# One hybrid decoder layer on one core: decode steps beside five heads, a norm product put later, the last squares taken by feature, and the values of seven heads turned by memory and VectorE

## The chip, the cores and the metric

One core of a Trainium2 chip runs the whole program. The metric is device time in microseconds of one launch. The kernel before was timed three times: 1744.43, 1745.99 and 1748.09 us, with the median 1745.99. One more execution was profiled and took 1747.35 us; its span in the profile, first to last recorded event, is 1745.6 us.

The engines are called as the profile calls them: PE (TensorE matmul; PEld is its weight load), DVE (VectorE), ACT (ScalarE), POOL (GpSimd) and SP (SyncE, which issues nearly all DMAs from one queue, in order).

## The reference, cut to what matters

One layer for a prompt of 1024 tokens and, with the same weights, eight requests that decode one token each from given states. Two mixers stand side by side, eight HGRN2 heads and sixteen Mamba-2 heads in two groups; then a gated MLP, and a last RMSNorm.

```python
h = rmsnorm(x, w['norm1_w'])
proj = h @ w['w_in']                       # 1024 x 6672
q_r, f_r, i_r, g_r, z, xbc_r, dt_r = jnp.split(proj, splits, axis=-1)
f = lb + (1.0 - lb) * jax.nn.sigmoid(f_r.astype(f32))
k = 1.0 - f
q = jax.nn.silu(q_r.astype(f32))
o_a, S_h_new = hgrn2_mix(heads(q), heads(k), heads(i_r.astype(f32)), heads(log_f), S_h.astype(f32))
o_a = rmsnorm(o_a, w['hgrn_norm_w']) * jax.nn.silu(heads(g_r).astype(f32))
...
y, S_s_new = ssd_scan(X * dt[..., None], A * dt, Bh, Ch, S_s.astype(f32))
y = y.reshape(Bsz, L, D_SSM) * jax.nn.silu(z.astype(f32))
y = rmsnorm(y.reshape(Bsz, L, SSM_GROUPS, -1), w['ssm_norm_w'].reshape(SSM_GROUPS, -1))
x = x + jnp.concatenate([o_a, y], axis=-1) @ w['w_out']
...
x = x + (jax.nn.silu(gate) * val) @ w['w_down']
y = rmsnorm(x, final_norm_w)               # after the layer
```

Here `hgrn2_mix` is, per head and token, S = diag(f) S + k v^T and o = q S; `v` is i_r. All is float32.

## The kernel before, in words

**Layout.** Features lie on the 128 partitions and tokens along the free axis: 1024 prompt tokens and, behind them, 8 decode tokens (NT = 1032). A projection tile is 128 features by three chunks of 344 tokens. Each float32 product is made of three products of rounded halves (weights wh and wl, activations hh and hl), and so one input job is 8 x 3 x 3 = 72 matmuls of 344 columns.

**Order on PE.** PE's queue is written out by hand. Jobs (`in_job`, L303: z0 to z7 for the gate of the Mamba part; f, q, v, sg for each head; then the output jobs) are generators that yield after each matmul. Beside them runs a stream: `ssd(g)` for the two Mamba groups, then `head(h, t)` for the heads. A stream yields weights, and `drive` (L279) makes a share of the remaining matmuls between two of its yields, until the job that it is driven to is done. So head h's small work is spread over the jobs of head h+1 (head 7's over output jobs), and a head takes about 62 us. `after(n, work)` (L242) puts work n matmul steps later. The queues of the other engines, and SP's, are ordered by a scheduler; `tc.issue_after(x)` asks that an instruction be queued behind x.

**A head (`head`, L934).** Its prompt part works in chunks of 128 tokens: products of q, k with powers of the forget gates fill the matrix `am` level by level (banks a0 to a6 in four stages, made by `near`: 64 or 32 pairs of products of only 16 to 64 columns), then per chunk the states SS (kv product, L1069; chain L1072 to L1074) and o = am v + q SS (L1094 on). For kv and o the values are wanted with tokens on the partitions, `vt`: eight PE transposes into two banks `vtp` (L945) and two ACT copies (L946) at the head's start. The norm of o follows: squares, `hms`, `rstd_of`, a round through memory (`hr_d`, `spread_rstd` 16 steps later), and 48 steps later `scale_out` (L1119): two DVE products sg = sg x norm and the store `mix_d<-sg`. The head's decode part loads two state tiles `Sh`, scales them with f on DVE (L959), adds k v, stores them, and takes `od` (PE, L1048) with `qb`; `odr` (L1051) is its copy. The loads of Sh for head h+1 can go out when od of head h has read the tiles.

**Decode steps of the Mamba part.** Sixteen heads make eight steps j. Each loads Sd (states), Bb and Cb (B and C spread over the partitions, 512 KB each), scales Sd on ACT (8 instructions), makes Bb x and Sd + Bb on DVE (1024 columns each), stores Sd, multiplies by Cb on POOL and sums on DVE. Steps 0 and 1 are made by `ssm_decode` in the z jobs z4 and z6, steps 2 to 7 by `decode_beside` (L677) in heads 1 to 6 in three parts: `load` behind the head's state store (L963), `front` behind odr, `back` behind the decode copy od (L1104). After the fourth step of a group `decode_gate` and, 80 steps later, `decode_norm` (dg, L735 to L737; xdk, L730) finish it, for group 1 at the start of head 7.

**The end.** The last rows of the down projection run by quarters of the tokens in the order 3, 0, 1, 2. Per quarter eight products dn are added to x on DVE (L1567); then, per 128 tokens, eight transposes `fin` (L1574), two ACT squares with a row sum (L1576), root and reciprocal, and two scales: one on DVE and one on ACT and POOL, or both on DVE in the last quarter (c == 2).

## Time and profile before

| what | us |
|---|---|
| runs: lowest, median, highest | 1744.43, 1745.99, 1748.09 |
| the profiled execution, and its span | 1747.35, 1745.6 |
| PE busy (share of the span) | 1704.6 (98%) |
| DVE busy | 1094.0 (63%) |
| ACT busy | 782.0 (45%) |
| POOL busy | 487.7 (28%) |
| granted TensorE clock, mean | 0.996 |

A row of the timeline gives the start, how long it took, the engine, the line, the operation, output and inputs by tile name, shapes, and in brackets the idle time of the engine just before, with what ended it. "x8" stands for eight of a kind together; a plain float32 matmul is recorded twice. A row of the groups gives the count, the busy time and the mean of one in ns. A row of windows gives, for a stretch, its length, then busy time and count for PE, PEld, DVE, ACT and POOL, the granted clock, the mean busy share of the 16 DMA engines, and GB/s. Of DMA queues it gives packets, MB and the share of 16 engines' time. Matmuls overlap, so a matmul's own duration is longer than the step from one start to the next.

### The profile page before, as it was taken

To read this page: it belongs to the slowest core of one execution; us is meant where nothing else is said; L and a number is where in the kernel's file an instruction comes from. 1 tells how busy PE (TensorE), PEld (TensorE's weight loads), DVE (VectorE), ACT (ScalarE), POOL (GpSimd) and SP (SyncE) were. 2 spreads that over 40 slices of the span, in tenths; PEclk is the share of its full clock that TensorE was granted. 3 is DMA by queue.
4 is the path that set the end of the run, shared out by engine and by line. 5 is a ranking of instruction groups with operands and counts; after the bars stand their busy time and mean duration, and the time that the engine had idled before them with its cause. 6 is when DMAs were issued, how large, how long until landed. Compare 5 with 4: busy or idle time off the path is not lost. (4 is left out here: it accounts for less than half of the span.)

```text
span 1745.6 us, 38507 instructions
## 1 busy us (share of the span) xinstructions
PE 1704.6 (98%) x16119; PEld 1657.3 (95%) x16119; DVE 1094.0 (63%) x1979; ACT 782.0 (45%) x1427; POOL 487.7 (28%) x501
## 2 busy tenths in 40 slices
PE   7999999999999999999999989999999999999998
PEld 7999999899989999999999989999999999999997
DVE  6668666555754655567746688666767667444545
ACT  7677685344445444445333464333334434111114
POOL 2102131110210211111122266666666664000002
PEclk9999999999999999999999999999999999999999
DMA  5354334533442443345437722222222226422212
GB/s 165 73 123 123 92 91 146 157 90 101 137 127 64 137 123 99 112 141 155 138 125 244 239 81 78 82 96 74 74 73 81 79 97 214 154 71 79 94 61 98
DMA packets 250036, 200.22 MB, mean 115 GB/s; under 512 B 47972, under 2 KB 221526, under 8 KB 249846
## 3 DMA queue, kind: packets, MB, share of 16 engines
q1 hardware_dynamic: 249574, 197.67, 37.4%
q8 instruction: 126, 2.06, 0.5%
q14 instruction: 48, 0.39, 0.1%
q0 software_dynamic: 288, 0.10, 0.0%
HBM read 155.16 MB, written 46.95 MB: 116 GB/s over the span
## 5 line engine op out<-in xcount | busy, mean ns | idle before, releaser
L93 PE MATMUL mm<-hl,wh 128*128 128x344 f32 x1248 | 405.2, 325 | 0.0
L93 PE MATMUL mm<-hh,wh 128*128 128x344 f32 x1248 | 404.9, 325 | 0.0
L93 PE MATMUL mm<-hh,wl 128*128 128x344 f32 x1248 | 402.0, 322 | 0.0
L93 PEld LDWEIGHTS mm<-hl,wh 128*128 128x128 f32 x1248 | 235.3, 189 | 4.8 <-issue 4.1
L93 PEld LDWEIGHTS mm<-hh,wh 128*128 128x128 f32 x1248 | 235.3, 189 | 4.0 <-issue 3.4
L93 PEld LDWEIGHTS mm<-hh,wl 128*128 128x128 f32 x1248 | 235.4, 189 | 1.4 <-issue 1.2
L199 ACT CAST wh<-ws 128x1024 fp32r<-128x1024 f32 x96 | 100.6, 1048 | 260.7 <-PE dn L93 134.8
L93 PE MATMUL ub<-uh,wh 128*128 128x258 f32 x704 | 200.1, 284 | 3.8 <-DVE fext L1432 2.7
L93 PE MATMUL ub<-ul,wh 128*128 128x258 f32 x704 | 199.5, 283 | 0.0
L93 PE MATMUL ub<-uh,wl 128*128 128x258 f32 x704 | 199.4, 283 | 0.0
L93 PE MATMUL dn<-ah,wh 128*128 128x256 f32 (+1 forms) x640 | 181.2, 283 | 2.0 <-DVE x L1549 2.0
L93 PE MATMUL dn<-al,wh 128*128 128x256 f32 (+1 forms) x640 | 180.6, 282 | 0.0
L93 PE MATMUL dn<-ah,wl 128*128 128x256 f32 (+1 forms) x640 | 180.1, 281 | 0.0
L201 DVE TENSOR_TENSOR wl<-ws,wh 128x1024 fp32r<-128x1024 f32 x88 | 109.7, 1247 | 93.3 <-ACT wh L199 92.6
L93 PE MATMUL mm<-mh,wh 128*128 128x258 f32 x512 | 146.5, 286 | 4.1 <-DVE x L1179 4.0
L93 PE MATMUL ua<-uh,wh 128*128 128x258 f32 x528 | 149.5, 283 | 0.8 <-DVE val L1444 0.4
L93 PE MATMUL ua<-ul,wh 128*128 128x258 f32 x528 | 149.2, 282 | 0.0
L93 PE MATMUL ua<-uh,wl 128*128 128x258 f32 x528 | 148.4, 281 | 0.0
L93 PE MATMUL mm<-ml,wh 128*128 128x258 f32 x512 | 145.3, 284 | 0.6 <-DVE ml L1136 0.6
L93 PE MATMUL mm<-mh,wl 128*128 128x258 f32 x512 | 144.9, 283 | 0.0
L93 PEld LDWEIGHTS ub<-uh,wh 128*128 128x128 f32 x704 | 133.6, 190 | 4.4 <-DVE fext L1432 2.9
L1382 DVE TENSOR_TENSOR wl<-wt,wh 128x512 fp32r<-128x512 f32 x88 | 89.4, 1035 | 74.2 <-ACT wh L1381 74.2
(373 smaller groups left out, 3987.4 us busy)
## 6 DMA issues: line engine op xcount, KB each, us to landing
ws<-in_w_in_dram SPq DMA_DIRECT2D x52, 512.0 KB
ws<-in_w_up_dram SPq DMA_DIRECT2D x44, 512.0 KB
ws<-in_w_out_dram SPq DMA_DIRECT2D x24, 512.0 KB
act_d<-val SPq DMA_DIRECT2D x22, 516.0 KB
al<-act_d SPq DMA_DIRECT2D x22, 516.0 KB
ws<-in_w_down_dram SPq DMA_DIRECT2D x22, 512.0 KB
ml<-mix_d SPq DMA_DIRECT2D x48, 172.0 KB
csb<-cs_d SPq DMA_DIRECT2D x32, 256.0 KB
```

The lines of the kernel that those rows point to most:

```text
L93: PE.matmul(out, lhsT, rhs, start=start, stop=stop)
L199: A.copy(wh[:, :n], ws[:, :n])
L201: V.tensor_tensor(wl[:, :n], ws[:, :n], wh[:, :n].bitcast(F32), op=ALU.subtract)
L1382: V.tensor_tensor(lo[:, cs], sums[name], hi[:, cs].bitcast(F32), op=ALU.subtract)
```

## The change

It has five parts.

1. **Values.** For heads 0 to 6 the job of v ends with four stores of v to memory `vb_d` (`v_end`), in pieces of 32 tokens, so that each block of 32 x 32 lands in the place of its transposed block. In the head the two `vt` tiles are loaded from there, queued behind the store of the second Sh, and two DVE transposes (of 32 x 32 blocks, in place), queued behind the odr copy, finish them. The PE transposes and ACT copies stay in head 7 only.
2. **Decode steps.** `decode_beside` runs in heads 1 to 5, for steps 3 to 7; step 2 is a third `ssm_decode`, and the three stand in z4, z5 and z6. Its load waits for the od matmul, its front is queued behind the od copy and square, its back behind `rstd_of`.
3. **Norm product.** `scale_out` of heads 0 to 6 is kept back and issued in the next head behind its odr copy.
4. **ssd's last yield** is 3.0 and not 1.0.
5. **The end.** In the last quarter (c == 2) ACT squares x by feature as each m is done, DVE adds the squares to `fa`, two matmuls of one column with ones give the sums of the rows, and one root and one reciprocal serve both halves; DVE makes three of the four scales and ACT with POOL the fourth.

```diff
@@ -686,8 +686,10 @@
         def load(behind):
-            with tc.issue_after(behind.ins):
-                SP.dma_start(d8(Sd), state_ssm[0, :, 2 * j:2 * j + 2].rearrange("b h p n -> (h p) b n"))
+            first_ = SP.dma_start(d8(Sd), state_ssm[0, :, 2 * j:2 * j + 2].rearrange("b h p n -> (h p) b n"))
+            tc.add_manual_dep(first_.ins, behind.ins.name,
+                              mybir.DependencyInfo(mybir.DependencyClass.Sync, mybir.DependencyReason.DATA))
+            with tc.issue_after(first_.ins):
                 SP.dma_start(Bb, bc_d[2 * g].rearrange("b n -> (b n)").unsqueeze(0).to_broadcast([P, T]))
@@ -734,7 +736,7 @@
         V.scalar_tensor_tensor(tmp, tmp, -0.5 / n, dst, op0=ALU.mult, op1=ALU.mult)
-        V.scalar_tensor_tensor(dst, tmp, 1.5, dst, op0=ALU.add, op1=ALU.mult)
+        return V.scalar_tensor_tensor(dst, tmp, 1.5, dst, op0=ALU.add, op1=ALU.mult)
@@ -747,8 +749,8 @@
                     acc.append(tl("g", "gacc"))
-                if g and i % 2 == 0:
-                    ssm_decode(0, i // 2)
+                if g and i < 3:
+                    ssm_decode(0, i)
@@ -818,7 +820,7 @@
         ssd_back(parts, NC - 1)
-        yield 1.0
+        yield 3.0
         ssm_state_out(g)
@@ -848,6 +850,7 @@
     vd_d = dram.tile([H, ND, P], F32, name="vd_d")
+    vb_d = dram.tile([H - 1, P, NC, P], F32, name="vb_d")
     hr_d = dram.tile([H, 4, 256], F32, name="hr_d")
@@ -918,6 +921,12 @@
+        def v_end():
+            for b in range(4):
+                SP.dma_start(vb_d[h, :, :, 32 * b:32 * b + 32].rearrange("(a j) c r -> j c a r", j=32),
+                             t["v"][32 * b:32 * b + 32, :T].rearrange("j (c a r) -> j c a r", a=4, r=32))
+
+        ends = {"f": f_end, "v": v_end if h < H - 1 else None}
         for n, off, func in (("f", OFF_F, AF.Tanh), ("q", OFF_Q, AF.Silu), ("v", OFF_I, AF.Copy),
@@ -929,17 +938,23 @@
             else:
-                in_job(f"{n}{h}", off + h * P, evict, begin, f_end if n == "f" else None)
+                in_job(f"{n}{h}", off + h * P, evict, begin, ends.get(n))
         return t
+
+    unscaled = []
...
         f, k, q, v, sg = (t[n] for n in ("f", "k", "q", "v", "sg"))
-        step_ = decode_beside((h + 1) // 4, (h + 1) % 4) if 1 <= h <= 6 else None
-
+        step_ = decode_beside((h + 2) // 4, (h + 2) % 4) if 1 <= h <= 5 else None
+
+        later_vt = []
         dps = bank("vd", "nx")
...
         for hf in range(2):
+            if h < H - 1:
+                later_vt.append((vt[hf], vb_d[h, :, 4 * hf:4 * hf + 4, :]))
+                continue
             ps = bank("vtp")
@@ -958,10 +973,12 @@
             G.tensor_tensor(Sd, Sd, vb, op=ALU.add)
-            kept_ = SP.dma_start(hgrn_sample[0, bs, h].rearrange("b k v -> k b v"), d4(Sd))
+            stored = SP.dma_start(hgrn_sample[0, bs, h].rearrange("b k v -> k b v"), d4(Sd))
             Sds.append(d4(Sd))
-        if step_:
-            step_[0](kept_)
+
+        for dst, src in later_vt:
+            with tc.issue_after(stored.ins):
+                SP.dma_start(dst.rearrange("p (c n) -> p c n", n=P), src)
@@ -1041,16 +1058,22 @@
             A.copy(am[b:b + 32, :, b + 32:b + 64], c32(ps[:, :256])[b:b + 32])
-        turned_ = A.copy(am[0:64, :, 64:P], p6[0:64, :].rearrange("p (c t) -> p c t", t=64))
+        A.copy(am[0:64, :, 64:P], p6[0:64, :].rearrange("p (c t) -> p c t", t=64))
...
             g = b % 4
-            mm(ops[32 * g:32 * g + 32, :P], qb[:, b, :], Sds[b // 4][:, b % 4, :], start=(b < 4), stop=(b >= 4))
+            oded = PE.matmul(ops[32 * g:32 * g + 32, :P], qb[:, b, :], Sds[b // 4][:, b % 4, :], start=(b < 4), stop=(b >= 4))
+        if step_:
+            step_[0](oded)
         odr = small.tile([P, P], F32, tag="odr", bufs=1, name=nm("odr"))
-        held = V.tensor_copy(odr, ops[:, :P])
-        if step_:
-            step_[1](held, turned_)
+        copied = V.tensor_copy(odr, ops[:, :P])
+        if h < H - 1:
+            for hf in range(2):
+                with tc.issue_after(copied.ins):
+                    V.transpose(vt[hf], vt[hf])
+        if unscaled:
+            unscaled.pop()(copied)
         yield 3.5
@@ -1079,10 +1102,10 @@
         held = V.tensor_copy(od[:, 0, :], dps[:, :ND])
-        A.activation(od[:, 1, :], dps[:, :ND], AF.Square)
+        turned_ = A.activation(od[:, 1, :], dps[:, :ND], AF.Square)
+        if step_:
+            step_[1](held, turned_)
         yield 3.2
-        if step_:
-            step_[2](held)
@@ -1105,7 +1128,9 @@
         nt = half("nt")
-        rstd_of(nt[:, 0:256], nt[:, 256:512], ps[:, :256], P)
+        held = rstd_of(nt[:, 0:256], nt[:, 256:512], ps[:, :256], P)
+        if step_:
+            step_[2](held)
         SP.dma_start(hr_d[h], nt[::32, 0:256])
@@ -1116,13 +1141,19 @@
-        def scale_out():
+        def scale_out(behind=None):
             for hf in range(2):
-                V.tensor_tensor(sg[:, hb[hf]], sg[:, hb[hf]], sq[hf], op=ALU.mult)
+                with ExitStack() as order_:
+                    if behind is not None:
+                        order_.enter_context(tc.issue_after(behind.ins))
+                    V.tensor_tensor(sg[:, hb[hf]], sg[:, hb[hf]], sq[hf], op=ALU.mult)
             SP.dma_start(mix_d[h], sg[:, :NT])
...
         after(16, spread_rstd)
-        after(48, scale_out)
+        if h < H - 1:
+            unscaled.append(scale_out)
+        else:
+            after(48, scale_out)
@@ -1560,32 +1591,63 @@
         wd.append((hi, lo))
+    def opened(t0, n):
+        tb = [bank("fin"), bank("fin")]
+        return t0, n, tb, [tl("t", "ot"), tl("t", "ot")], keep.tile([P, 6], F32, tag="ss", bufs=4, name=nm("fss"))
+
+    def turned(o, ks):
+        t0, n, tb, ot, ss = o
+        for k in ks:
+            PE.transpose(tb[k // 4][:n, blk[k % 4]], xT[k][:, t0:t0 + n], ident)
+
+    def scaled(o, i, r, shared):
+        t0, n, tb, ot, ss = o
+        ds = slice(i * 512, (i + 1) * 512)
+        if shared:
+            A.activation(ot[i][:n], tb[i][:n, :], AF.Copy, scale=r)
+            G.tensor_tensor(ot[i][:n], ot[i][:n], fw[:n, ds], op=ALU.mult)
+        else:
+            V.scalar_tensor_tensor(ot[i][:n], tb[i][:n, :], r, fw[:n, ds], op0=ALU.mult, op1=ALU.mult)
+        SP.dma_start(y_prompt[0, t0:t0 + n, ds] if t0 < T else y_sample[:, 0, ds], ot[i][:n])
+
     for c in (3, 0, 1, 2):
         cs = quarters[c]
+        parts_ = [(t0, min(P, cs.stop - t0)) for t0 in range(cs.start, cs.stop, P)]
+        acc_ = tl("us", "fa")[:, :256]
         for m in range(KT):
...
             V.tensor_tensor(xT[m][:, cs], xT[m][:, cs], ps, op=ALU.add)
...
+            if c == 2:
+                q_ = tl("us", "fq")[:, :256] if m else acc_
+                A.activation(q_, xT[m][:, cs], AF.Square)
+                if m:
+                    V.tensor_tensor(acc_, acc_, q_, op=ALU.add)
+        if c == 2:
+            os_ = [opened(t0, n) for t0, n in parts_]
+            for o in os_:
+                turned(o, range(KT - 1))
+            sums = psmm.tile([P, 512], F32, tag="mm", name=nm("fs"))
+            for b in range(2):
+                mm(sums[:, b:b + 1], acc_[:, blk[b]], ones[:, 0:1])
+            for o in os_:
+                turned(o, range(KT - 1, KT))
+            r = os_[0][4]
+            A.activation(r[:, 0:2], sums[:, 0:2], AF.Sqrt, bias=epsc, scale=1.0 / DM)
+            V.reciprocal(r[:, 2:4], r[:, 0:2])
+            for b, i in ((0, 0), (0, 1), (1, 0), (1, 1)):
+                scaled(os_[b], i, r[:, 2 + b:3 + b], (b, i) == (1, 1))
+        else:
+            for t0, n in parts_:
+                o = opened(t0, n)
+                tb, ot, ss = o[2:]
+                turned(o, range(KT))
...
+                for i in range(2):
+                    scaled(o, i, ss[:n, 3:4], i == 1)
```

How the queues change. First VectorE's queue in the middle of the fourth head, from the decode copy odr to the last state step, before (sg_6165 is that head's gate tile, Sd_6300 and Bb_6301 its Mamba step, Sh_7128 and Sh_7136 the next head's states):

```order
L1051 COPY odr_6825<-od_6816 128x128
L698 TENSOR_TENSOR Bb_6301<-Bb_6301,xdd_6299 128x1024
L950 TENSOR_TENSOR qb<-eye_796,q_6614 128x8x8
L702 TENSOR_TENSOR Sd_6300<-Sd_6300,Bb_6301 128x1024
L959 TENSOR_TENSOR Sh_7128<-Sh_7128,f_6354 128x512
L959 TENSOR_TENSOR Sh_7136<-Sh_7136,f_6354 128x512
L1072 COPY SS_6917<-kv_6918 128x128
L1074 SCALAR_TENSOR_TENSOR SS_6917<-SS_6917,tt_6345,kv_6918 128x128 x2
```

and the same place of the changed kernel (sg_5386 is the gate tile of the head before):

```order
L1070 COPY odr_6838<-od_6825 128x128
L1074 STREAM_TRANSPOSE vt_6343<-vt_6343 128x512
L1074 STREAM_TRANSPOSE vt_6344<-vt_6344 128x512
L1149 TENSOR_TENSOR sg_5386<-sg_5386,sq_6222 128x512
L1149 TENSOR_TENSOR sg_5386<-sg_5386,sq_6234 128x512
L965 TENSOR_TENSOR qb<-eye_796,q_6623 128x8x8
L974 TENSOR_TENSOR Sh_7138<-Sh_7138,f_6377 128x512
L974 TENSOR_TENSOR Sh_7146<-Sh_7146,f_6377 128x512
L1095 COPY SS_6921<-kv_6922 128x128
L1097 SCALAR_TENSOR_TENSOR SS_6921<-SS_6921,tt_6368,kv_6922 128x128
```

The transposes and the held-back products stand where Bb and Sd stood; Bb is now behind the second and Sd behind the fifth of the seven state steps.

SyncE's queue at that place, before, where Sd, Bb and Cb had gone out right behind the stores of Sh of the head's first part:

```order
L961 DMA out_dram<-Sh_6324 128x4x128
L961 DMA out_dram<-Sh_6332 128x4x128
L690 DMA Sd_6300<-in_state_ssm_dram 128x8x128
L691 DMA Bb_6301<-bc_d 128x1024
L693 DMA Cb_6302<-bc_d 128x512
L693 DMA Cb_6303<-bc_d 128x512
L196 DMA ws_6968<-in_w_in_dram 128x8x128
L182 DMA Sh_7128<-in_state_hgrn_dram 128x4x128
L182 DMA Sh_7136<-in_state_hgrn_dram 128x4x128
```

and of the changed kernel (from the first Sh on, all wait for od):

```order
L976 DMA out_dram<-Sh_6357 128x4x128
L981 DMA vt_6343<-vb_d 128x512
L981 DMA vt_6344<-vb_d 128x512
L182 DMA xd_6394<-in_x_sample_dram 8x512
L182 DMA xd_6395<-in_x_sample_dram 8x512
L196 DMA ws_6990<-in_w_in_dram 128x8x128
L182 DMA Sh_7138<-in_state_hgrn_dram 128x4x128
L689 DMA Sd_6337<-in_state_ssm_dram 128x8x128
L693 DMA Bb_6338<-bc_d 128x1024
L695 DMA Cb_6339<-bc_d 128x512
L695 DMA Cb_6340<-bc_d 128x512
L1150 DMA mix_d<-sg_5386 128x1032
```

The next row is the second Sh (Sh_7146): the two loads of Sh, which stood together, now have the Mamba step's loads and the store of the gate tile between them.

VectorE's queue at the start of head 7, before (dg and xdk finish the Mamba group, sg_8532 is head 6's gate tile):

```order
L1009 TENSOR_TENSOR v_9181<-q_8961,f_8715 128x1024
L1121 TENSOR_TENSOR sg_8532<-sg_8532,sq_9331 128x512
L986 TENSOR_TENSOR tt_9472<-f_8715 128x512
L1121 TENSOR_TENSOR sg_8532<-sg_8532,sq_9343 128x512
L201 TENSOR_TENSOR wl_9478<-ws_9476,wh_9477 128x1024
L1136 TENSOR_TENSOR ml_9489<-ml_9489,mh_9485 128x344 x2
L986 TENSOR_TENSOR tt_9473<-tt_9472 128x256
L735 SCALAR_TENSOR_TENSOR dg_9319<-dgs_9545,dg_9319 128x8
L980 TENSOR_TENSOR k_8952<-k_8952,f_8715 128x512
L736 SCALAR_TENSOR_TENSOR dg_9319<-dg_9319 128x8
L981 TENSOR_TENSOR v_9181<-v_9181,f_8715 128x512
L737 SCALAR_TENSOR_TENSOR dg_9319<-dg_9319 128x8
```

and of the changed kernel:

```order
L1026 TENSOR_TENSOR v_9179<-q_8968,f_8714 128x1024
L1003 TENSOR_TENSOR tt_9463<-f_8714 128x512
L1003 TENSOR_TENSOR tt_9464<-tt_9463 128x256
L1003 TENSOR_TENSOR tt_9464<-tt_9464 128x128
L201 TENSOR_TENSOR wl_9469<-ws_9467,wh_9468 128x1024
L1167 TENSOR_TENSOR ml_9480<-ml_9480,mh_9476 128x344 x2
L1033 TENSOR_TENSOR amc_9465<-a_1069_9544,eyec 128x256
L1003 TENSOR_TENSOR tt_9464<-tt_9464 128x64
L997 TENSOR_TENSOR k_8959<-k_8959,f_8714 128x512
L998 TENSOR_TENSOR v_9179<-v_9179,f_8714 128x512
```

The two products on sg and the three steps on dg are gone from here, and three short squarings tt stand ahead of k.

PE's queue differs only in the first Mamba rows of the start, in the 56 transposes that are gone, in the group's closing product (in head 6 and not in head 7), and at the very end.

28 lines of the change are left out of this document (6 added, 22 removed).

## The prediction

> **What bounds the kernel now.** I read four things in this order: the page's busy shares, the list of everything TensorE waits for, the timeline around those waits, and the DMA queues inside them.
>
> ```profile
> span 1745.6 us, 38507 instructions
> PE 1704.6 (98%) x16119; PEld 1657.3 (95%) x16119; DVE 1094.0 (63%) x1979; ACT 782.0 (45%) x1427; POOL 487.7 (28%) x501
> ```
>
> PE is busy 98% of the span. So only two things can shorten it: fewer PE instructions, or a shorter wait of PE; work moved on VectorE, ScalarE or SyncE's queue counts only where PE waits for it. PE's waits in the part that the change touches (waited for: total, times, longest):
>
> ```profile
> PE a L93 <- issue: 5.2, 3, 2.5
> PE sT L636 <- DVE S L611: 2.3, 1, 2.3
> PE a L93 <- DVE q L981: 2.3, 1, 2.3
> PE mm L93 <- DVE ml L1136: 0.6, 1, 0.6
> ```
>
> That is 10.4 us in six waits, and they are what an edit off PE can win here.
>
> **Values by memory: the transposes that go.** One head's start on PE, then all of them, and the ScalarE copies behind them:
>
> ```profile
> 372.58 0.27 PE L940 MATMUL vd<-ident,v 128*8 128x128 f32 x1
> 372.69 1.03 PE L945 MATMUL vtp<-ident,v 128*128 128x128 f32 x8
> 373.48 0.40 PE L93 MATMUL mm<-hh,wh 128*128 128x344 f32 x1
> L945 PE MATMUL vtp<-ident,v 128*128 128x128 f32 x64 | 8.3, 272 | 0.0
> L946 ACT COPY vt<-vtp 128x512 f32<-128x512 f32 x16 | 8.6, 594 | 0.0
> ```
>
> The 272 ns are the time in flight of one transpose, not its price: eight occupy 1.03 us. The price is start to start. From 372.58 (vd) to the next projection row at 373.48 stand nine transposes in 0.90; the ninth projection row starts somewhat late, by the 0.40 of its own row, so I take 0.11 each, 0.87 for eight. Seven heads lose theirs: **-6.1 us** (by 0.10 it would be -5.6, by 0.12 -6.7). The two ScalarE copies per head (2 x 594 ns) hide today beside projections and win nothing.
>
> The Trainium skill, "TensorE: Matmul & The Clock Gate", Part 4, gives a transpose about 275 ns in a kernel's context, and the trace's mean of 272 agrees. Multiplied by 56 this would be an estimate of -15.4 us, but the starts in the row above are 0.11 apart, so I go by those.
>
> What comes instead runs beside PE: four stores of 128 KB and two loads of 256 KB a head, and two VectorE transposes. A store in such 128-byte pieces exists already (x_prompt to its copy), and so does the transpose:
>
> ```profile
> 54.00:56.00 2.00, 2.00 (x20) 2.00 (x18) 2.00 (x2) 1.72 (x2) 0.00 (x0) 1.00 0.74 116
> L901 DVE STREAM_TRANSPOSE xs<-xs 128x512 f32<-128x512 f32 x16 | 11.2, 704 | 10.5 <-DMA xs<-xb_d 10.5
> ```
>
> 116 GB/s at a DMA share of 0.74 make 155 GB/s at full share: 512 KB take 3.4 us. They start when the job of v ends, over ten us before the next head begins, and the values are first read by that head's kv product some 40 us into it; the loads go out 14 us into it. I see no wait there: 0. The 2 x 0.70 on VectorE come up below.
>
> **The three waits named "issue".** These are the largest item, and the diff has no line about them. Their rows, and the DMA queues (packets, MB, share) of the whole run, of 512.0 to 519.5 and of 519.5 to 521.0:
>
> ```profile
> 390.26 0.19 PE L93 MATMUL a<-q,f 128*32 128x32 f32 x1 [0.77 <-issue]
> 518.60 0.76 PE L93 MATMUL a<-q,f 128*32 128x32 f32 x64
> 519.21 0.55 PE L93 MATMUL a<-v,k 128*16 128x16 f32 x48
> 522.25 0.29 PE L93 MATMUL a<-v,k 128*16 128x16 f32 x16 [2.49 <-issue]
> 649.51 0.21 PE L93 MATMUL a<-v,k 128*16 128x16 f32 x2 [1.92 <-issue]
> q8 instruction: 126, 2.06, 0.5%
> ```
> ```profile
> q1 hardware_dynamic: 2331, 2.02, 94.7%
> ```
> ```profile
> q8 instruction: 1, 0.02, 3.7%
> ```
>
> 2.06 MB in 126 packets are 16 KB each, and PE's 2 x 16119 instructions are 126 x 256: the packets are PE's instructions, 256 at a time. The counts between the stalls say the same:
>
> ```profile
> 390.20:522.20 132.00, 129.47 (x1784) 123.88 (x1783) 76.78 (x138) 57.52 (x98) 14.71 (x10) 1.00 0.42 125
> 522.20:649.50 127.30, 125.34 (x1656) 120.27 (x1656) 73.17 (x142) 60.89 (x106) 17.77 (x12) 0.99 0.38 111
> ```
>
> 1784 + 1783 = 3567 and 1656 + 1656 = 3312 recorded instructions; with the 16 or 17 semaphore instructions of PE between them these are 14 x 256 and 13 x 256. So each stall sits on a packet's border. It is a border that falls at the end of the burst of small "a" products (64 and 64 pairs of weight load and product, in some 1.3 us without the stall), at a moment when the data queue is full: for 7.5 us at a share of 0.95 no instruction packet moved at all, then one came and PE went on. The data are the store of Sh, Sd, Bb, Cb and a weight tile, 2.4 MB issued 14 us into heads 2 and 4.
>
> The change touches both conditions. Every head has 16 PE instructions fewer, so the border at 522.25 moves 48 instructions on (the burst had 32 left) and that at 649.51 80 on (4 left): both leave the burst. And 1.5 MB of the data (Sd, Bb, Cb) go out behind od instead, so the queue empties some 4.5 us sooner. Other borders come into bursts: I counted all of them in the changed order, and six have 5.1 to 5.6 us from the border before to the end of their packet, against the 4.7 to 5.5 of those that stalled; the queue is nearly empty at four. I take 5.2 of stalls gone and 0.6 new: **-4.6** (ends: 0, all reappear, and -5.2).
>
> The Trainium skill, "Runtime: NRT & Kernel Launch", Instruction fetch mechanics, has the same blocks of 16 KiB, 256 instructions, but calls the cost of crossing one mostly hidden. By that rule the stalls would have another cause and stay, and the sum would be 4.6 us higher.
>
> **Head 7 is relieved.** VectorE at its start, with the wait that PE has there:
>
> ```profile
> 813.30 0.69 DVE L1121 TENSOR_TENSOR sg<-sg,sq 128x512 f32<-128x512 f32 x1
> 818.78 1.00 DVE L736 SCALAR_TENSOR_TENSOR dg<-dg 128x8 f32<-128x8 f32 x1
> 820.31 1.25 DVE L737 SCALAR_TENSOR_TENSOR dg<-dg 128x8 f32<-128x8 f32 x1
> 821.82 0.63 DVE L730 SCALAR_TENSOR_TENSOR xdk<-xdk,vcol,dg 128x8 f32<-128x8 f32 x4
> 822.97 0.68 DVE L981 TENSOR_TENSOR q<-v,tt 128x512 f32<-128x512 f32 x1
> 823.80 0.93 PE L93 MATMUL a<-q,f 128*32 128x32 f32 x53 [2.33 <-DVE q L981]
> ```
>
> VectorE has no pause from 812 to 824, and the q that PE waits for is at its end. Two norm products (2 x 0.6 start to start) go behind od, and the group end of the decode (0.9 + 1.2 + 0.5) to head 6, whose start has the same work but one output job less beside it. That is 3.8 us out of a chain that is 2.33 late; the three tt halvings that now come ahead cost some 0.5. So -2.3, and the 0.63 for ml goes with the norm product: **-2.9** (ends 0 and -2.9). The same 2.1 now stand at head 6's start, where PE had no wait: 0, at most +1.
>
> **The decode behind od.** Here the change adds a danger. The rows of head 3:
>
> ```profile
> 595.38 0.64 PE L93 MATMUL od<-Sh,qb 128*32 128x128 f32 x16
> 595.86 0.94 SPq L182 DMA_DIRECT2D Sh<-in_state_hgrn_dram  x2
> 605.76 0.29 DVE L1072 COPY SS<-kv 128x128 f32<-128x128 f32 x1 [3.35 <-PE kv L93]
> L702 DVE TENSOR_TENSOR Sd<-Sd,Bb 128x1024 f32<-128x1024 f32 x6 | 7.4, 1225 | 0.4 <-ACT Sd L701 0.3
> 613.93 0.39 PE L93 MATMUL o<-q,SS 128*128 128x128 f32 x2
> 512.00:519.50 7.50, 7.50 (x146) 7.04 (x147) 4.54 (x8) 4.23 (x6) 0.00 (x0) 1.00 0.95 269
> 760.00:773.00 13.00, 13.00 (x322) 12.49 (x321) 8.74 (x14) 5.47 (x8) 2.73 (x2) 1.00 0.69 204
> ```
>
> SyncE issues now, behind od: Sh, Sd, Bb, two Cb, the store of sg, and only then the second Sh, 2.62 MB in all where it was 0.5. VectorE's queue has the scaling of that Sh ahead of COPY SS, so the whole chain of states waits for it. At the 269 GB/s of just such loads it lands 9.7 us on, with one to two for the first to start at 606.6 to 607.6; the scaling takes 1.2, so COPY SS starts near 608.3 instead of 605.76. From there SS6 comes 4.5 us later (six small steps of some 0.3, and Bb and Sd of 1.1 each between them): 612.8. PE reads it for its last product of o, 0.45 behind the row at 613.93, at 614.4. So 1 to 2 us are left, and I count **+0.3** for the five heads. VectorE's time beside it balances: two transposes and two norm products (2.7) for Bb and Sd (2.4), under a pause of 3.35. The third ssm_decode in the z jobs brings ScalarE and SyncE a wait for Sd where none bound PE; ends 0 and 3, I take **+0.5**. The yield of 3.0 in place of 1.0 changes no row of PE's order at sT, so the 2.3 there stay.
>
> **The end.** Before, behind the last dn:
>
> ```profile
> 1736.21 0.42 DVE L1567 TENSOR_TENSOR x<-x,dn 128x256 f32<-128x256 f32 x1 [0.28 <-PE dn L93]
> 1736.64 0.60 ACT L1576 ACTIVATE ot<-fin 128x512 f32<-128x512 f32 x1 [1.91 <-PE fin L1574]
> 1738.95 1.41 DVE L1586 SCALAR_TENSOR_TENSOR ot<-fin,fss,fw 128x512 f32<-128x512 f32 x2
> 1741.05 1.41 DVE L1586 SCALAR_TENSOR_TENSOR ot<-fin,fss,fw 128x512 f32<-128x512 f32 x2
> ```
>
> ScalarE's row squares (four of 0.60 and their sums) and two rounds of root and scale go. If only the last dn counted, x at 1736.21, square, add, two products, root, reciprocal and three scales of 0.7 would end 5.0 behind it against 6.3 now: -1.3. But VectorE gets seven adds of 0.36 in the last quarter, beside eight x adds of 0.36, two scales of 0.75 and small ones: 7.7 us from 1731.2, where PE takes 5. It comes out some 2 late: **+0.65** (ends -1.3 and +1.5).
>
> **The sum**, against the profiled execution's 1747.35 (1.75 outside the span, 1.36 above the median of 1745.99): -6.1 - 4.6 - 2.9 + 0.3 + 0.5 + 0.65 = -12.1, which is 1735.2 in the profile and 1733.8 as a median. I predict **1734**, 0.7% faster.
>
> **Rivals.** (a) The instruction stalls reappear at other borders: five heads now have a fuller queue, though behind od, where no burst stands, which speaks against it; or they have a cause that the change doesn't touch, and stay. Then 4.6 are missing: 1738 to 1740. The Trainium skill's page named above stands for the second of these. (b) The second Sh comes at the 204 GB/s of the row at 760, whose share is only 0.69: 12.8 + 1.5 us, 1.6 too late, five times: +8, or 1743. (c) The other side: the queue behind od gives only 158 GB/s, as it moved over 595.9 to 606.0 before (at a share of 0.57, so mostly unasked, which speaks against it). Then Sh lands after 18.1 us, 5.4 beyond the 12.7 that it has, in five heads: +27, or 1761. It turns slower than before when it lands later than about 15 us behind od, 2.4 a head. (d) VectorE bounds the end: at most 1737.
>
> **Chances.** Forecast, with (d) in it: 0.54, 1731 to 1738. (a) 0.20; (b) 0.14; (c) 0.12. The measurement tells about 0.2%, 3.5 us: faster below 1742.5 is 0.54 + 0.20, same is nearly all of (b), slower is (c). The range of eight in ten reaches from the forecast's low end, 1731, over (a) and most of (b) to 1745.
>
> **What would show it.** PE's count falls by 56 transposes and no "issue" wait over 1 us stands in the bursts of heads 2 and 4: the first two steps. No wait of PE on q near 820: the third. A wait of o on SS in heads 1 to 5, with VectorE's Sh waiting for its load: (b) or (c), and the prediction is wrong. An "issue" wait elsewhere, again a multiple of 256 from the others: (a). The span's end less the last dn tells the tail.

## The result, and the profile after

| | lowest | median | highest | runs |
|---|---|---|---|---|
| before, us | 1744.43 | 1745.76 | 1752.49 | 6 |
| after, us | 1749.70 | 1753.99 | 1756.36 | 6 |

The changed kernel is slower: 1.0043 of the kernel before, 95% interval 1.0026 to 1.006. The forecast was 1734 with a range of 1731 to 1745: the change went the other way, and the time lies above the range. The profiled execution of after took 1756.36, its span is 1754.6, 9.0 more than before's.

The page's head, after:

```profile
span 1754.6 us, 38477 instructions
PE 1705.6 (97%) x16067; PEld 1656.6 (94%) x16067; DVE 1098.2 (63%) x1998; ACT 779.4 (44%) x1416; POOL 483.3 (28%) x502
```

PE has 52 rows fewer (56 transposes less, 4 rows of the products fs more), yet its busy time rose by 1.0. So it did less work in more time, and waited more besides. What PE waited for (total, times, longest), after:

```profile
PE mm L93 <- ACT x L1208: 4.8, 1, 4.8
PE cst L346 <- DMA rt<-in_state_conv_ffn_dram: 4.5, 1, 4.5
...
PE a L93 <- issue: 2.8, 3, 1.4
...
PE sT L636 <- DVE S L611: 2.5, 1, 2.5
...
PE mm L93 <- issue: 1.4, 2, 1.1
...
PE fin L1601 <- DVE x L1619: 1.1, 2, 0.7
...
PE o L93 <- DVE SS L1097: 0.7, 1, 0.7
```

Two waits of over 4 us are new, and neither is in the prediction. The wait of 2.33 for q in head 7 is down to 0.21, as forecast. "Issue" came down from 5.2 to 2.8 + 1.4 = 4.2, not to 0.6. The two new ones in PE's timeline, after:

```profile
518.26 0.42 PE L346 MATMUL cst<-ident,rt 16*128 16x16 f32 x4 [4.50 <-DMA rt<-in_state_conv_ffn_dram]
...
833.77 0.58 PE L93 MATMUL mm<-mh,wh 128*128 128x258 f32 x1 [4.80 <-ACT x L1208]
```

**The first: rows of a state, late in SyncE's queue.** `rt` are small loads of the MLP's convolution state that PE turns (L346) between two heads' work. SyncE's queue around them, before:

```profile
498.20 0.34 SPq L182 DMA_DIRECT2D rt<-in_state_conv_ffn_dram  x1
...
502.46 0.43 SPq L182 DMA_DIRECT2D rt<-in_state_conv_ffn_dram  x1
...
508.07 3.22 SPq L961 DMA_DIRECT2D out_dram<-Sh  x2
...
514.27 0.44 SPq L182 DMA_DIRECT2D rt<-in_state_conv_ffn_dram  x1
```

and after:

```profile
510.05 3.52 SPq L976 DMA_DIRECT2D out_dram<-Sh  x2
513.62 0.99 SPq L981 DMA_DIRECT2D vt<-vb_d  x2
514.65 1.37 SPq L182 DMA_DIRECT2D rt<-in_state_conv_ffn_dram  x3
```

Before, the rows went out one at a time, two of them ahead of the stores of Sh. After, three stand together behind the stores of Sh (which wait for POOL's sums, so SyncE's queue stands still until 510) and behind the new loads of `vt`. They went out at 514.65 and PE had them at 518.26. The diff asks only that vt stand behind the store of Sh; in an in-order queue whatever the scheduler puts behind vt is held back with it. How the 4.5 divide isn't shown: the stores of Sh hold the rows until 513.6, the loads of vt take another 1.0 of SyncE's queue, and while the rows were under way (514.65 to 518.2) the DMA engines were busy at a share of 0.75.

**The second: ScalarE's evictions behind its casts.** The output job beside head 7 needs `ml` (the mixed heads, from memory), which ScalarE casts to `mh`. ScalarE, after:

```profile
829.00 0.94 ACT L1166 CAST mh<-ml 128x344 fp32r<-128x344 f32 x2 [3.00 <-DMA ml<-mix_d]
830.98 1.44 ACT L1166 CAST mh<-ml 128x344 fp32r<-128x344 f32 x3 [1.04 <-DMA ml<-mix_d]
...
833.36 0.36 ACT L1208 COPY x<-mm 128x258 f32<-128x258 f32 x1
```

`COPY x<-mm` empties the bank that PE waits for, and it is a third of a microsecond of work. It stands behind five casts that wait for loads of ml, and behind two copies for the head. In before, the Mamba part's store `mix_d<-xdk` goes out at 822.47, behind head 7's stores of Sh, and the loads of ml follow from 823.69 on. In after it went out at 765.98, a head earlier, and SyncE issues the loads of ml at 817.6, at 822.1 and from 825.3 on: before, between and behind the two stores of Sh, which wait for POOL. That the earlier store is why the scheduler placed the loads and casts among the evictions is my reading of the two orders; the run x_mix below tests only the place behind the stores of Sh.

**The clock, which the prediction left out.** Stretches behind those waits (length, busy times and counts of PE, PEld, DVE, ACT, POOL, then the granted clock, DMA share, GB/s), after:

```profile
518.00:520.00 2.00, 1.74 (x9) 1.72 (x10) 0.57 (x2) 0.00 (x0) 0.00 (x0) 0.66 0.00 0
520.00:524.00 4.00, 4.00 (x21) 4.00 (x20) 1.39 (x4) 3.55 (x5) 0.00 (x0) 0.74 0.00 0
524.00:528.00 4.00, 4.00 (x147) 3.75 (x146) 1.43 (x3) 1.24 (x2) 0.00 (x0) 1.00 0.47 135
...
833.00:839.00 6.00, 5.23 (x143) 4.96 (x144) 5.68 (x12) 4.49 (x12) 0.00 (x0) 0.50 0.14 50
```

and before, behind the stall at 522.25 and the wait for q at 823.8:

```profile
522.00:528.00 6.00, 5.75 (x42) 5.50 (x42) 2.85 (x5) 2.22 (x5) 0.00 (x0) 0.72 0.02 5
...
823.00:828.00 5.00, 4.20 (x83) 4.17 (x84) 3.48 (x12) 1.16 (x3) 0.00 (x0) 0.66 0.67 173
```

Behind most long waits PE goes on at half the clock for a while. The trace's clock record has these stretches at exactly 0.5, each 3.41 us long or, in some, 6.83 (in b_vals below once 10.24). The one in before at 522:

```profile
523.00:526.40 3.40, 3.40 (x14) 3.40 (x13) 2.47 (x5) 1.22 (x2) 0.00 (x0) 0.50 0.02 5
```

By the rows above, the slow stretches of before cost 6.0 x 0.28 = 1.7 and 5.0 x 0.34 = 1.7. Those of after cost 2.0 x 0.34 + 4.0 x 0.26 = 1.7 at 518, 6.0 x 0.50 = 3.0 at 833, and another 1.6 behind sT (below). A fall behind a wait of 2.7 at 1040 stands in both profiles. So a wait of PE has two prices, the wait and the slow stretch behind it, and the second is not listed among the waits.

**The end**, PE of after:

```profile
1745.55 1.10 PE L1601 MATMUL fin<-ident,x 128*128 128x128 f32 x7 [0.75 <-DVE x L1619]
1747.13 0.74 PE L93 MATMUL fs<-ones,fa 128*128 128x1 f32 x4 [0.47 <-DVE fa L1624]
```

VectorE is behind. The last dn of after starts at 1742.99 and the span ends 11.6 later, against 9.7 before.

### The profile page after: what moved, and what is told of

It is laid out like the page before. It is cut to its first block, busy times and chain, and to the rows that moved or that the text cites. A ratio compares the mean times of both kernels' runs of the same rounds, so it can differ in the third digit from the quotient of the medians.

```text
span 1754.6 us, 38477 instructions
## 1 busy us (share of the span) xinstructions
PE 1705.6 (97%) x16067; PEld 1656.6 (94%) x16067; DVE 1098.2 (63%) x1998; ACT 779.4 (44%) x1416; POOL 483.3 (28%) x502
## 5 line engine op out<-in xcount | busy, mean ns | idle before, releaser
L201 DVE TENSOR_TENSOR wl<-ws,wh 128x1024 fp32r<-128x1024 f32 x88 | 114.9, 1306 | 85.6 <-ACT wh L199 85.4
L93 PEld LDWEIGHTS ub<-ul,wh 128*128 128x128 f32 x704 | 134.3, 191 | 0.0
```

The source lines that it names most:

```text
L93: PE.matmul(out, lhsT, rhs, start=start, stop=stop)
L201: V.tensor_tensor(wl[:, :n], ws[:, :n], wh[:, :n].bitcast(F32), op=ALU.subtract)
```

## Experiments

Each run was timed beside the kernel before on the same chip, in five rounds; ratios are to that. The waits come from each kernel's profile. Theory at the start: the queue of SyncE, ScalarE's evictions and the clock took the gain back. Rival: the forecast gains were not there.

**Values alone (b_vals).** The kernel before, with the values of heads 0 to 6 by memory and nothing else of the change.

```diff
+            for b in range(4):
+                SP.dma_start(vb_d[h, :, :, 32 * b:32 * b + 32]..., t["v"][32 * b:32 * b + 32, :T]...)
...
-            ps = bank("vtp")
+            if h < H - 1:
+                later_vt.append((vt[hf], vb_d[h, :, 4 * hf:4 * hf + 4, :]))
+                continue
...
+                with tc.issue_after(held.ins):
+                    V.transpose(vt[hf], vt[hf])
```

> The kernel before with the values of heads 0 to 6 by memory alone: 56 transposes less on PE, all else as it was. Theory V1: PE's order loses 0.87 us a head, 6.1 in all, and nothing else waits, save that the packet borders move: 3 to 8 us less than before, 0.2 to 0.45%. Rival V2 (the stores and loads of v delay SyncE's queue and with it other loads): a wait of PE for a load appears, and the time is that of before or more.

Measured: 1755.97, ratio 1.0042 [1.003, 1.0055], as slow as the whole change. PE and VectorE of this kernel at the start of head 2:

```profile
514.57 0.75 PE L93 MATMUL a<-q,f 128*32 128x32 f32 x64 [2.75 <-DVE q L995]
...
523.01 0.57 PE L346 MATMUL cst<-ident,rt 16*128 16x16 f32 x4 [6.86 <-DMA rt<-in_state_conv_ffn_dram]
```
```profile
511.15 1.34 DVE L1139 TENSOR_TENSOR sg<-sg,sq 128x512 f32<-128x512 f32 x2 [5.36 <-DMA sq<-hr_d]
```

The wait for rt is there, and longer: the values' part makes it by itself. Here it is not the queue's order alone. The last rows of rt went out at 515.91 to 516.88 and PE had them at 523.01, behind the loads of vt, Sd, Bb and Cb, with the DMA engines busy at a share of 0.92 from 514.8 to 522.8. The wait for q has another cause. The norm product of the head before stands in VectorE's queue ahead of q and waits 5.36 for its load sq. That load went out at 503.90, 8.5 us later than in before (495.41), because the steps of the norm (nt) stand further back in two queues. Its root on ScalarE comes at 497.12, behind an eviction that waits 4.10 for PE, and its steps on VectorE come from 499.45 on, behind a copy that waits 8.98 for PE:

```profile
495.35 0.46 ACT L931 ACTIVATE sg<-mm 128x344 f32<-128x344 f32 x1 [4.10 <-PE mm L93]
...
499.25 0.28 DVE L959 COPY vd<-vd 8x128 f32<-8x128 f32 x1 [8.98 <-PE vd L948]
```

In before the root came at 491.79 and the steps at 492.30, ahead of both. So the edit of the values' path changed the order that the scheduler made for ScalarE and VectorE as well. The change has moved just this norm product behind odr, so its parts lean on each other, and b_vals shows one without the other.

**The two mends (x_rt, x_mix, x_both).** The changed kernel with rt held two loads ahead; with head 7's stores of Sh issued behind its od; with both.

```diff
-        nxt = rows(0)
+        ahead = 2 if ntile > XT else 1
+        nxt = [rows(j) for j in range(0, 4 * ahead, 4)]
...
-            (rt, nj), nxt = nxt, rows(j0 + 4) if j0 + 4 < ntile else None
+            rt, nj = nxt.pop(0)
+            if j0 + 4 * ahead < ntile:
+                nxt.append(rows(j0 + 4 * ahead))
```
```diff
-            stored = SP.dma_start(hgrn_sample[0, bs, h]...)
+            if h < H - 1:
+                stored = SP.dma_start(hgrn_sample[0, bs, h]...)
...
+        if h == H - 1:
+            for b0 in (0, 4):
+                st_ = SP.dma_start(hgrn_sample[0, b0:b0 + 4, h]..., Sds[b0 // 4])
+                tc.add_manual_dep(st_.ins, oded.ins.name, ...)
```

> The changed kernel with the small state loads rt fetched two blocks ahead, so that the third stands in SyncE's queue ahead of the stores of Sh that wait for POOL. Theory 1 (order of the queue): the wait of PE for rt at 518 us (4.5) goes, and with it the stretch of halved clock behind it (2 us lost): 5.5 to 7 us less than the changed kernel, 1747 to 1749. Theory 2 (the memory stores and loads of v fill the DMA, and rt is slow wherever it stands): rt still lands late, at most 2 us less. Theory 3 (the low clock is a state of its own and not tied to the wait): 4.5 less, and a stretch at a clock of 0.5 stays near 520.

> The changed kernel with the two stores of Sh of head 7 put behind its od product, so that the loads ml of the second output block don't stand behind them in SyncE's queue. Theory 1 (order of SyncE's and ScalarE's queues: ScalarE's rounding of ml waits for those loads, with PE's evictions behind it): the wait of PE on ScalarE's copy x at 833 us (4.8) goes with its stretch of halved clock (2.7): 6 to 8 us less, 1746 to 1748. Theory 2 (the DMA is full there): at most 2 us less. Theory 3: 4.8 less and the slow clock stays.

> Both mends together. Theory 1: the sum, 12 to 14 us less than the changed kernel, 1740 to 1742, so about 5 us or 0.3% faster than before: what the change was to win less the instruction waits, the first halving of the clock at 316 us and the end. Theory 2: 1750 or more. Theory 3: 1744 to 1746.

Measured: x_rt 1753.35, 1.0033 [1.0021, 1.0046]; x_mix 1752.04, 1.0025 [1.0014, 1.0037]; x_both 1750.92, 1.0005 [0.9988, 1.0021]. Each wait goes or shrinks where its mend is: in x_rt that for rt is gone, in x_mix that for the eviction falls from 4.80 to 2.58. But each of the two alone had been expected to save 5.5 to 8 us, and neither can be told from the change by itself, whose interval is 1.0026 to 1.006. The eviction of x_mix:

```profile
831.02 0.39 PE L93 MATMUL mm<-mh,wh 128*128 128x258 f32 x1 [2.58 <-ACT x L1214]
```

Both together make the change neutral. They do not bring the 12 to 14 us that theory 1 expected of them, in part because another wait steps in at the start of head 2. PE of x_both, and its VectorE before it:

```profile
514.26 1.08 PE L93 MATMUL a<-q,f 128*32 128x32 f32 x64 [2.88 <-DVE q L1002]
```
```profile
508.04 0.17 DVE L740 SCALAR_TENSOR_TENSOR dg<-dgs,dg 128x8 f32<-128x8 f32 x1 [1.78 <-ACT dg L739]
508.24 0.17 DVE L741 SCALAR_TENSOR_TENSOR dg<-dg 128x8 f32<-128x8 f32 x1
508.44 1.26 DVE L742 SCALAR_TENSOR_TENSOR dg<-dg 128x8 f32<-128x8 f32 x1
509.74 2.44 DVE L735 SCALAR_TENSOR_TENSOR xdk<-xdk,vcol,dg 128x8 f32<-128x8 f32 x4
```

With the steps moved a head forward, a group of decode steps now ends at the start of head 2. VectorE waits there 1.78 for ScalarE, then works 4 us on the group's end, all ahead of q. In the changed kernel q stands ahead of all but the first of these steps, and PE had no wait for it (`a<-q,f` ran at 512.17, before the wait for rt). VectorE of after:

```profile
510.49 1.53 DVE L998 TENSOR_TENSOR q<-v,tt 128x512 f32<-128x512 f32 x1
```

Its last dg and the xdk came at 514.30 to 515.1. So the delay was not there, hidden, in the changed kernel: in the two runs with rt held two ahead, x_rt and x_both, the scheduler made another order for VectorE, and x_rt has this wait too (2.90). The `a` row is 1.08 long against 0.75 for the same 64 products in b_vals: the clock was halved (0.50 over the next 4 us).

**Do the stalls at instruction packets only move? (b_shift.)** The kernel before with 64 more PE instructions ahead of sT, transposes of 8 x 8 that nothing reads.

```diff
+        if g == 1:
+            for _ in range(32):
+                PE.transpose(ps[:8, :8], ident[:8, :8], ident[:8, :8])
```

> The kernel before with 32 transposes of 8 x 8 more on PE in its wait at sT (64 instructions, some 2 us inside a wait of 2.3), nothing else. Theory of the instruction packets: every border lies 64 instructions earlier in the program, the three issue waits at 390, 522 and 649 us leave their places; no border with a short packet then falls into the two stretches of full DMA, and 0 to 1.5 us of such waits are left in the heads: 4 to 7 us less than before, with the stretch of halved clock at 522 gone, 1739 to 1742. Rival (the small products or the full DMA stall PE themselves, wherever the packet borders are): the waits stay within 1 us of their places in the program and the time is that of before.

Measured: 1749.76, 1.0008 [0.9996, 1.0021]. The stalls at 390, 522 and 649 are gone; others of 0.75 to 2.25 stand at 463, 516, 591 and 773:

```profile
463.18 0.32 PE L93 MATMUL mm<-hl,wh 128*128 128x344 f32 x1 [1.00 <-issue]
...
516.23 0.25 PE L93 MATMUL a<-q,f 128*32 128x32 f32 x3 [1.09 <-issue]
...
591.04 0.32 PE L93 MATMUL mm<-hh,wh 128*128 128x344 f32 x1 [0.75 <-issue]
...
773.00 0.42 PE L93 MATMUL mm<-hh,wh 128*128 128x344 f32 x1 [2.25 <-issue]
```

They come to some 5, as before. That the stalls sit on borders of 256 instructions holds: moving every border by 64 moved every stall, and counted with weight loads and semaphores the three stalls of before and the four of b_shift all lie at a multiple of 256, plus 193. In after the three long ones (1.06 at 393.73, 1.10 at 582.02, 1.36 at 765.26) lie at PE instructions 5569, 10433 and 15297, which are 21, 40 and 59 times 256, plus 193. That a border moved out of a burst takes the stalls away for good fails, since other borders stall. Nor need the border lie in the burst: those at 463 and 591 stand among projection rows, 4 us behind one (457.90 to 459.2, 585.65 to 587.0). Nor need the data queue be full. The four microseconds of after that end in its stall at 582.02, at a DMA share of 0.25 and 0.30:

```profile
578.00:580.00 2.00, 1.87 (x53) 1.52 (x55) 0.00 (x0) 0.09 (x1) 1.92 (x3) 1.00 0.25 70
580.00:582.00 2.00, 0.92 (x99) 0.81 (x88) 0.00 (x0) 0.00 (x0) 0.98 (x1) 1.00 0.30 84
```

**The end alone, and the old end (b_end, x_end).** b_end is the kernel before with the changed last quarter; x_end is x_both with the old one.

```diff
-            for i in range(2):
-                A.activation(ot[i][:n], tb[i][:n, :], AF.Square, accum_out=ss[:n, i:i + 1])
+                A.activation(q_, xT[m][:, cs], AF.Square)
+                if m:
+                    V.tensor_tensor(acc_, acc_, q_, op=ALU.add)
```

> The kernel before with the new end alone (squares of the last quarter feature-major, one root and one reciprocal for both parts). The prediction counted +0.65 (from -1.3 to +1.5). Theory E1 (VectorE's eight added sums make it late at the end, so the tail is 2.0 to 2.4 longer, as in every kernel with this end): span's end less the last dn about 2 us longer than before's, ratio 1.0008 to 1.0018. Rival E2 (the tail is longer only beside the other edits): within 0.7 us of before, ratio 0.9995 to 1.0005.

> Both mends, and the end as it was before (squares by row, on ScalarE). From the last dn to the span's end the four kernels with the new end take 2.0 to 2.4 us more than before. Theory E1 (VectorE's seven more additions in the last quarter are what ends late): the end is 9.6 us behind the last dn again, 2 us less than with both mends alone, some 0.1% under the kernel before. Rival E2 (the end is late because something before it, the last stores, ends late): no change.

Measured: b_end 1747.81, 1.0 [0.9991, 1.001]; x_end 1748.49, 1.0001 [0.9988, 1.0014]. From the last dn's start to the span's end it is 9.7 in before and 9.7 in b_shift and b_fill, which have before's end and before's values; 10.0 in b_vals and b_vrt, with the values by memory; 10.3 to 10.4 in the five mended kernels with the old end (x_end, x_z567, x_dgs, x_best, x_fill); 10.6 in b_end; 11.6 to 11.9 in after, x_rt, x_mix and x_both. So alone the end costs about 0.9 in its profile and nothing that the runs can tell; beside the other edits 1.2 to 2.2. My theory of 2 us everywhere fell. The old end too grows beside the other edits, by 0.3 to 0.7; why stays open.

**Head 0 and head 2 (x_z567, x_dgs, x_best).** x_end with the early decode steps in z5 to z7 (x_z567); that with the group's end put 140 steps behind and not 80 (x_dgs); and the second edit alone (x_best).

```diff
-                if g and i < 3:
-                    ssm_decode(0, i)
+                if g and i > 0:
+                    ssm_decode(0, i - 1)
```
```diff
-        after(80, lambda: decode_norm(g, js, dg))
+        after(140, lambda: decode_norm(g, js, dg))
```

> As the last, with the three decode steps of the Mamba part in z5, z6 and z7 instead of z4, z5 and z6. PE's wait at sT (2.4 to 2.9 us in all kernels with the change, 2.34 before) stands behind VectorE's product with Bb, which waits for its load. Theory S1: with that step one job later the product isn't ahead of S in VectorE's queue, the wait falls under 1 us and the clock is not halved at 316 us: 3 to 4 us less than the run before it here. Rival S2 (S waits for its own product, not for Bb): the wait stays and with it the time. Rival S3: the third step is then late for the first head, with a new wait of PE near 390 us.

> As the last, with the closing norm of a Mamba group 140 matmul steps behind its last decode step and not 80. In head 2 PE waits 2.9 us for q at 514 us behind VectorE's closing steps, with 2 us of halved clock. Theory H1: moved out of the chain, that wait falls under 0.5: 4 to 5 us less than the run before it, 0.5% under the kernel before in all, 1736 to 1739. Rival H2 (VectorE is full in head 2 whatever stands there): the wait stays within 1 us.

> The changed kernel with the conv state's rows fetched two ahead, head 7's two stores of Sh behind its od, the old end, and decode_norm after(140), but with the decode steps in z4 to z6 as the change has them (the first version that has every mend and not the a<-q waits of head 0 that the move to z5 to z7 brought). Theory T1 (each part's saving is real on PE, and what took it back are queues that can be mended): the waits at head 2's start, at the conv state and at ml are under 1 us each, no wait over 1 us at 385 to 400; transposes -6.1, head 7's q -2.3, less 'issue' stalls of 3 to 5 us as before: ratio 0.9955 to 0.9975 (about 1741 to 1744). Rival T2 (PE's saved time is always taken by the next thing that is late): ratio 0.999 to 1.001, with new waits of together 5 us or more besides 'issue' and sT.

Measured: x_z567 1750.58, 1.0011 [0.9999, 1.0023]; x_dgs 1746.75, 0.9994 [0.9981, 1.0006]; x_best 1745.54, 0.9988 [0.9978, 0.9999]. In x_z567 the wait at sT is gone (S1), but head 0 pays for it (S3). Its PE and VectorE:

```profile
397.10 1.08 PE L93 MATMUL a<-q,f 128*32 128x32 f32 x64 [3.92 <-DVE q L1002]
```
```profile
393.85 1.28 DVE L794 SCALAR_TENSOR_TENSOR xbc<-xbc,vcol,gacc 128x1024 f32<-128x1024 f32 x1 [3.72 <-DMA gacc<-gr_d]
```

The later group end of x_dgs takes away the wait for q in head 2, and x_best has that gain without the waits in head 0. Its ratio is no more than 0.2% under before and fits neither theory (up to 0.9975; from 0.999 on), though it comes nearer to the second. The waits left in its profile in this part are sT 2.7, "issue" 3.1 + 1.2 and an eviction 2.6.

**Values with both mends, nothing else (b_vrt).** b_vals with rt two ahead and the group's end at 140.

> The kernel before with the values of heads 0 to 6 by memory (as b_vals), and the two mends for what b_vals showed: conv state's rows two ahead and decode_norm after(140). Theory V1 (the values' part gains its 6 us on PE once SyncE's queue and VectorE's start of head 2 are mended): the wait of 6.9 for rt and that of 2.8 for q in head 2 are gone, ratio 0.9965 to 0.9985 (the q wait of 2.1 in head 7 and 4 to 5 us of 'issue' stay). Rival V2 (the loads and stores of the values delay something else in turn): 0.9995 to 1.002, with another wait over 2.5 us at a start of a head or at sT.

Measured: 1750.54, 1.0011 [0.9999, 1.0024]. The wait for rt is gone; 2.37 for q in head 2 stays (VectorE's norm product again, 4.97 for its load), and an "issue" stall of 2.22 and an eviction of 2.96 are new. So the second theory held, in its time and in new waits of this size. That the moved norm product is what the values' part lacks here is argued from the wait for q; no run has these two parts alone.

**Does the wait cause the slow clock? (x_fill, x_fillT, b_fill, a_fill.)** Two products that nothing reads (four recorded rows, 1.9 us), put where PE waits for VectorE in front of sT, into the bank that sT overwrites: in x_best (x_fill), in before (b_fill) and in after (a_fill). x_fillT puts sixteen 128 x 128 transposes there instead, in x_best.

```diff
         ps = bank("sT")
+        if g == 1:
+            for _ in range(2):
+                mm(ps, BT[g][:, 0:P], CT[g][:, 0:512])
```

> x_best with two products (128x512, into the bank that the transposes of sT then overwrite) issued in front of sT of the second group, where PE waits some 2.5 us for VectorE. They compute nothing that is read. Theory C1 (the clock halves because PE runs no product for over some 2.3 us): the wait at sT splits into two pieces under 1.5 us, and the granted clock stays 1.00 over the next 4 us (in runs with a gap of 2.5 there it fell to about 0.5 to 0.65): about 1.5 us less than x_best if that has the halving, 0.999 of it. Rival C2 (the fall is caused by something else at that place, not by the gap): the clock falls to 0.5 to 0.7 behind sT as before.

> x_best with sixteen 128x128 transposes (some 1.8 us) in place of x_fill's two products in front of sT. Theory F1 (transposes do not count for the clock as products do; in b_shift 32 small ones were followed by a fall to 0.69): clock at 0.5 to 0.7 behind sT, ratio as x_best's, 0.998 to 0.9995. Rival F2 (a full-size transpose counts like a product): clock 1.00 behind sT, ratio 0.996 to 0.9975 as x_fill's.

> The kernel before with the two products in front of sT, which nothing reads. Theory C1 (the wait without a product makes the clock fall, in many executions at sT, and the filler ends that): no wait over 1 us at sT, clock 1.00 over the next 4 us, ratio 0.9975 to 0.9992 (the profile of before happened to show no fall at sT, other kernels with its code up to there did, 1.7 us each). Rival C2 (x_fill gained by where the packets' borders fell, which the filler moves by 8 instructions, not by the clock): ratio 0.9995 to 1.0005, whatever the clock at sT does, and the sum of the waits named issue differs from before's 5.2 by over 2 us in x_fill's direction only there.

> The changed kernel with the same two products and no mend. Theory C1: the fall behind sT goes (it cost 1.7 in the profile of the changed kernel), the waits of 4.5 for the conv state's rows and 4.8 for ml's eviction stay, each with its own fall: ratio 1.0022 to 1.0035, one to three us less than the changed kernel's 1.0043. Rival C2: 1.004 to 1.005.

Four microseconds behind sT in after, with 17 PE rows in it:

```profile
316.40:320.40 4.00, 3.90 (x17) 3.90 (x18) 4.00 (x9) 3.71 (x7) 1.34 (x1) 0.61 0.23 66
```

The same in x_fill, with the filler's row ahead of it:

```profile
314.20:318.20 4.00, 3.90 (x27) 3.87 (x27) 4.00 (x9) 3.69 (x7) 1.33 (x1) 1.00 0.25 66
```
```profile
312.35 1.88 PE L93 MATMUL sT<-xbc,xbc 128*128 128x512 f32 x4
```

and in x_fillT:

```profile
315.70:319.70 4.00, 3.91 (x26) 3.91 (x27) 4.00 (x9) 3.73 (x7) 1.34 (x1) 1.00 0.23 66
```

PE is equally busy in all three stretches, and at a clock of 0.61 it gets 17 rows done where it does 26 or 27. Of the ten profiles with a bare wait of 2.34 to 2.87 at sT eight show the fall, 0.50 to 0.65 over the next 4 us; of the four with a filler none. In b_shift, where the 8 x 8 transposes stood there, 1.89 of the wait was left and the fall came (0.62). So the wait without work causes the fall, at this place. Full-size transposes held the clock as the products did, as F2 had it, in one profile: had they not counted, PE would have been without work for 3.1 us there, and each of the 18 waits of 2.79 and more behind the program's first was followed by a fall.

The times: x_fill 1741.17, 0.9968 [0.9957, 0.9979]; x_fillT 1742.46, 0.9965 [0.9952, 0.9977]; b_fill 1747.2, 1.0001 [0.9987, 1.0015]; a_fill 1754.49, 1.0036 [1.0022, 1.0051]. x_fill and x_fillT beat both kernels, the fastest versions of this study. But in before the filler gains nothing measurable (C1 was right on the clock, and C2's ratio came out; before's own profile had no fall at sT to begin with), and in after 0.07%, within the intervals: a_fill's profile has no fall at sT, but waits of 4.7 for rt and 5.3 for the eviction. That x_fill lies 4 us under x_best is more than the 1.6 of one fall, and x_best's profile is the other of the two without a fall at sT. Between their two profiles the difference comes from several places: the wait at sT (2.75, in its place 1.9 of products that nothing reads); a shorter wait for the eviction in head 7 (1.7 against 2.6); and the fall behind that eviction, the only one of x_best before the end, which x_fill does not have. So what the filler gains by the clock at sT, these times do not show.

## Why the prediction was wrong

The terms of its sum against the two profiled executions, in us:

| term | forecast | measured |
|---|---|---|
| transposes of seven heads | -6.1 | -6.1 |
| "issue" stalls | -4.6 | -1.0 (5.2 to 4.2) |
| head 7: q and ml | -2.9 | -2.7 (2.33 to 0.21, and 0.6 gone) |
| second Sh behind od | +0.3 | +0.7 (one wait) |
| third ssm_decode | +0.5 | 0, no wait found |
| the end | +0.65 | +1.9 (9.7 to 11.6) |
| values' loads and stores on SyncE | 0 | +4.5 (rt) |
| evictions beside head 7 | 0 | +4.8 |
| slow clock behind waits | not counted | +2.9 (1.6 + 1.7 + 3.0 less 1.7 + 1.7) |
| other waits: x evictions, start, sT | 0 | +1.9 (1.3, 0.5, 0.1) |

That sums to +6.9 of the span's +9.0; 2.1 are in no wait that I can name.

**Transposes: right.** In after one vd and the next projection row start 0.03 apart, where there were 0.90:

```profile
375.30 0.27 PE L952 MATMUL vd<-ident,v 128*8 128x128 f32 x1
375.33 0.40 PE L93 MATMUL mm<-hh,wh 128*128 128x344 f32 x1
```

That is 0.87 a head. The price start to start held, not the 272 ns in flight. The estimate of -15.4 from the 275 ns of the Trainium skill ("TensorE: Matmul & The Clock Gate", Part 4) did not come.

**The step that failed: the values' stores and loads, "I see no wait there: 0".** I worked out how long 512 KB take and when the values are read, and was right: no head waited for `vt`. (One slip: 116 GB/s at a share of 0.74 make 157 GB/s at full share and not 155, which changes nothing here.) What I left out is that a DMA put into SyncE's queue, fenced behind a store that waits for POOL, holds back the transfers behind it that have nothing to do with values. The order of SyncE's rows, which shows rt falling behind Sh and vt, could be read before the run; I read it only for Sh, Sd, Bb and Cb. b_vals shows a wait of 6.9 for rt with the values' part alone, a part of it for the data that stand ahead, and x_rt removes it.

**"Issue": the borders right, the conditions wrong.** The stalls do lie on borders of 256 instructions, and the borders of 522 and 649 left their bursts without a stall, as I had worked out. The step that failed is the 0.6 for other borders: they took 4.2. I had judged them by whether the border falls in a burst and how full the data queue would be, took it as nearly empty at four, and neither condition holds: the stall at 582 of after came at a DMA share of 0.25 to 0.30, two of b_shift among projection rows. The border at 390, which moves by 16 instructions only, stalled again (0.77 before, 1.06 after). What decides which border stalls stays open. b_shift shows the better estimate: where borders shift and the work stays, expect the total to stay, here 5. That is rival (a), at 0.20, and its first cause, other borders, though not by a fuller queue.

By the Trainium skill's "mostly hidden" ("Runtime: NRT & Kernel Launch", Instruction fetch mechanics) the stalls would have another cause and stay. They did not: after's, 1.1 to 1.4 each, have moved with the borders.

**Head 7: right for q, and a new wait behind it.** What I did not follow is that the loads and casts of the output job, on SyncE and ScalarE, move too when the group's end goes a head earlier with its store of `mix_d`. The 4.8 of this wait stand in no term of the sum.

**The decode behind od: right.** In head 3 of after the scaling of the second Sh starts 12.4 behind od, where I had 11.2 to 12.2; one wait of 0.67 for SS followed, in head 4. Rivals (b) and (c) did not happen.

**The end: rival (d) in part.** VectorE was late, as the sum of 7.7 against 5 said, and by more than I took.

**No term for the clock.** The wait at 823.80 and the stall at 522.25 that I quoted were followed by slow stretches in before (the stall at 649.51 was not: 1.00 over the next 4 us), in the same view that I used for the DMA share. Taking it in would have raised the gain of most waits removed and the price of most waits made.

## What to carry to other kernels

When a change adds DMAs to an in-order queue, list every transfer that now stands behind them or behind their fence, and price the first one that somebody waits for; bytes and bandwidth alone do not show it. Price a wait of a saturated PE with the slow stretch behind it, and do not book a stall as gone when its trigger only moves. A part that saves real time on the busiest engine (6 us here) can be worth nothing until the queues around it are put in order, so try it with its mends before judging it. An edit to one part can also change the order that a scheduler makes for other engines, so compare their queues, not only the edited one.
